# Strassen's seven products in the gated MLP of a hybrid encoder block on one core

## The chip, the core and the metric

The kernel runs on one core of a Trainium2 chip. The metric is the time of one execution on the device, in microseconds (us). The core has a matrix engine (TensorE, PE in the profile), three engines for elementwise work (VectorE or DVE, ScalarE or ACT, GpSimd or POOL), and DMA queues; here nearly all DMAs are issued by SyncE (SP). SBUF is the memory on the core, 128 partitions wide; PSUM holds the results of PE; DRAM lies outside. An engine runs its instructions in the order in which the program lists them, and waits on semaphores for the others.

## The reference

```
h = rmsnorm(x, norm_mix_g);  z = h @ w_in              # conv heads and latent attention
x = x + concat([y_conv, y_mla]) @ w_o
hf = rmsnorm(x, norm_ffn_g)
a  = dwconv_centred(hf @ w_up, ffn_conv_w, ffn_conv_b) # width 3, over positions
g, u = split(a, 2)
x  = x + (silu(g) * u) @ w_down
gate = sigmoid(rmsnorm(x, ple_norm_g) @ w_ple_gate)
x  = x + gate * (p @ w_ple_proj)
return rmsnorm(x, final_norm_g)
```

There are 1024 positions and 1024 channels. The MLP's inner width is 2816, so 22 chunks of 128 channels for g and 22 for u. The embedding p has 256 channels. Everything is float32.

## The kernel before

Activations lie with channels on the partitions and positions along the row: one tile is 128 channels by 1024 positions. Every matrix product is made of three passes over split operands. A weight w is split into a rounded part wh and the rest wl, an activation x into xh and xl, and a product is wh·xh + wh·xl + wl·xh (`gemm`, L127 to L134: L130, L132, L134). A matmul covers 128 by 128 weights and 512 positions. `load_unit` (L119) brings 1024 columns of weights from DRAM by a DMA of SP (L116), and splits them: ACT writes wh (L123), POOL the difference wl (L124). Three raw buffers let these run ahead of PE.

After the attention, its half of the output projection is made for each of eight chunks of channels, `out_mla`; DVE adds it to x (L555), ACT and DVE split the gained x (not yet normed) into hh and hl (L213, L214), and ACT and POOL gather the squares for the norm (L221, L222). `rbc` (L158) turns the sum of squares into the factor r2 by two matmuls with ones (L170, L171) and rsqrt steps on ACT and DVE (L151 to L156).

The MLP then runs without DRAM in between. For chunk c, `ff_chunk` makes two units of 48 matmuls, g and u, on hh and hl. PE does not need r2: DVE multiplies the PSUM result by it (L226), then come the width-3 convolution (ACT L203, DVE L204 and L205), silu on ACT (L574), and the product g·u on DVE (L577). The product is split by ACT and POOL (L209, L210) into guh and gul, which stay in SBUF. The down projection takes chunks in groups, GROUPS = [4, 4, 4, 4, 3, 3]: when a group and one further chunk have been made, eight blocks of n × 6 matmuls follow, one for each output chunk, and DVE adds each into x (L625). In the last group x is split again (L213, L214) for the gate.

The last stage works on parts of the positions, (0, 512), (512, 768), (768, 1024). For each output chunk PE makes the embedding projection (12 matmuls) and the gate (24 matmuls), then ACT, DVE and POOL apply the sigmoid, the sum and the final norm. The order of instructions on each engine comes from the order of the code, a scheduler, and the buffers of the pools, and is fixed when the program is built.

Of the kernel before, what the change touches and what calls it, by code (L numbers as in the profile page):

```python
# [14 lines left out]
P = 128  # L15
S = 1024
# [3 lines left out]
NFF = 22  # L20
EPS = 1e-6
SCALE = 96.0 ** -0.5
GROUPS = [4, 4, 4, 4, 3, 3]

POOLW = 256
ACTN = (0, 3, 6)
# [7 lines left out]
def tile_block(ctx, tc, xT, pT, wlat, wun, wdn, wuq, wukv, vecs, cst, out):  # L34
# [16 lines left out]
    ps = ctx.enter_context(tc.tile_pool(name="ps", bufs=2, space=bass.MemoryType.PSUM))  # L51
# [59 lines left out]
    def vc(i):  # L111
        return vec[:, i:i + 1]
# [11 lines left out]
        ptt(out=wl, in0=raw, in1=f(wh), op=ALU.subtract)  # L124
        return wh, wl

    def gemm(acc, wh, wl, xh, xl, first, last, sl=HALF):  # L127
        hv = acc if isinstance(acc, list) else halves(acc)
        for p, s in zip(hv, sl):
            mm(p, wh, xh[:, s], start=first, stop=False)  # L130
        for p, s in zip(hv, sl):
            mm(p, wh, xl[:, s], start=False, stop=False)  # L132
        for p, s in zip(hv, sl):
            mm(p, wl, xh[:, s], start=False, stop=last)  # L134
# [89 lines left out]
    def times(out_, acc, b):  # L224
        for p, s in pieces(acc):
            tt(out=out_[:, s], in0=p, in1=b[:, s], op=ALU.mult)  # L226

# [134 lines left out]
    yp, y_done = pool("yp", "right")  # L362
    atp, at_done = pool("atp", "right")
    YH = [yp.tile([P, S], FR, name=f"ymh{i}") for i in range(4)]
# [166 lines left out]
    xp, x_done = pool("xp", "left")  # L531
    x1 = [xp.tile([P, S], F32, name=f"x{c}") for c in range(NC_)]
    for d in range(NC_):
        nc.sync.dma_start(out=x1[d], in_=x1d[d])
# [11 lines left out]
    out_mla(1, [0, 1, 2])  # L546
    values(NT // 2 - 1)
    out_mla(2, [0, 1, 2])
    ss = xp.tile([P, S], F32, name="ss")
    hh = [xp.tile([P, S], FR, name=f"hh{c}") for c in range(NC_)]  # L550
    hl = [xp.tile([P, S], FR, name=f"hl{c}") for c in range(NC_)]
    for d in range(NC_):
        out_mla(d, [3] if d < 3 else [0, 1, 2, 3])
        for p, s in pieces(accs[d]):
            tt(out=x1[d][:, s], in0=p, in1=x1[d][:, s], op=ALU.add)  # L555
# [5 lines left out]
    gp, g_done = pool("gp", "right", 6)  # L561
    tmpb, tmpb_done = pool("tmpb", "right", 4)
    tpools = [tmp, tmpb]
    cnt = [0]

    r2 = [None]
    pend = []

    def ff_evac(c, j, acc, ab):
        a = ft()  # L570
        times(a, acc, r2[0])
        ab.append(conv3(a, V_FW + 3 * (2 * c + j), V_FB + 2 * c + j))
        if j == 0:
            act(out=ab[0], in_=ab[0], func=AF.Silu)  # L574
        else:
            g, u = ab
            tt(out=g, in0=g, in1=u, op=ALU.mult)  # L577
# [5 lines left out]
    def ff_chunk(c):
        ab = []
        tpool[0] = tmpb if c % 2 else tmp
        for j in range(2):
            acc = unit_gemm(U_UP + 2 * c + j, hh, hl, [small(), small()] if c == 1 and j == 0 else None)
            if r2[0] is None:
                pend.append((c, j, acc, ab))
            else:  # L590
                ff_evac(c, j, acc, ab)

    def set_r2(r):
        r2[0] = r
        while pend:
            ff_evac(*pend.pop(0))

    ph, wj = [], []

    def prep(src, lst):  # L600
        raw = load_raw(src)
        pair = (gp.tile([P, S], FR, name="guh"), gp.tile([P, S], FR, name="gul"))
        split(raw, *pair, nc.vector)
        lst.append(pair)

    done = {}
    rbc(ss, D, xp.tile([P, S], F32, name="rbc"), 9.0, set_r2)
    nxt = 0
    col = 0
    c0 = 0  # L610
    for g, n in enumerate(GROUPS):
        last = g == len(GROUPS) - 1
        ahead = c0 + n + 1 if g < len(GROUPS) - 2 else NFF
        while nxt < ahead:
            ff_chunk(nxt)
            nxt += 1
        for d in range(NC_):
            if last and d in (0, 1, 3):
                prep(*[(pT[0], ph), (pT[1], ph), None, (wun[U_PROJ], wj)][d])
            if d % 2 == 0:  # L620
                w = load_unit(wdn[:, col:col + 2 * n * P], 2 * n * P)
                col += 2 * n * P
            p = big()
            blocks(p, w, d % 2 * n, [done[c0 + k][0] for k in range(n)], [done[c0 + k][1] for k in range(n)], range(n), n)
            tt(out=x1[d], in0=p, in1=x1[d], op=ALU.add)  # L625
            if last:
                if d == 0:
                    ss = xp.tile([P, S], F32, name="ss")
                    hh, hl = [], []
                hh.append(xp.tile([P, S], FR, name=f"hh{d}"))  # L630
                hl.append(xp.tile([P, S], FR, name=f"hl{d}"))
                split_gain(x1[d], vc(V_PLE + d), hh[d], hl[d])
                square_acc(ss, x1[d], d == 0)
        c0 += n

# [1 line left out]
    prep(wun[U_PROJ + 1], wj)  # L637
    r3 = [None]
    gate_pend = []
    last_sq = []  # L640
    PARTS = [(0, 512), (512, 768), (768, 1024)]
    sf = [xp.tile([P, b - a], F32, name=f"sf{i}") for i, (a, b) in enumerate(PARTS)]

    def gate_evac(i, d, pg, pj):
        a, b = PARTS[i]
# [53 lines left out]
    rbc(ss, D, xp.tile([P, S], F32, name="rbc"), 8.0, set_r3)  # L699
    for i, (a, b) in enumerate(PARTS):  # L700
        s = slice(a, b)
        for d in range(NC_):
            w = load_unit(wun[U_GATE + d])
            if i == 0 and d in (2, 3):
                pg, pj = small(), small()
            elif i == 0:
                p = big()
                pg, pj = p[:, 0:512], p[:, 512:1024]
            else:
                p = small()  # L710
                pg, pj = p[:, 0:256], p[:, 256:512]
            for k in range(2):
                c = slice((d % 4 * 2 + k) * P, (d % 4 * 2 + k) * P + P)
                gemm([pj], wj[d // 4][0][:, c], wj[d // 4][1][:, c], ph[k][0], ph[k][1], k == 0, k == 1, [s])
            for k in range(NC_):
                c = slice(k * P, k * P + P)
                gemm([pg], w[0][:, c], w[1][:, c], hh[k], hl[k], k == 0, k == NC_ - 1, [s])
            if r3[0] is None:
                gate_pend.append((i, d, pg, pj))
            else:  # L720
                gate_evac(i, d, pg, pj)
        if b < S:
# [114 lines left out]
```

## Time and profile before

| | |
|---|---|
| median of three runs | 1410.96 us (1410.74 to 1413.64) |
| span of the profiled execution | 1409.6 us |
| instructions | 16320, of which 6612 matmuls |
| PE, DVE, ACT, POOL busy | 97%, 57%, 39%, 40% |
| the MLP (first matmul on hh to the first of the gate stage) | 528.0 to 1254.3 us |
| the gate stage | 1254.3 to 1409.6 us |

The page of the profile gives busy times, slices of the span, groups of instructions by line (busy time in us, mean of one in ns, then the idle time ahead of them and what ended it) and DMA issues. In rows of the timeline stand start, duration, engine, line, operation, output<-input and, in brackets, the idle time before it with its releaser. A row of the windows view gives a stretch, its length and the busy time of each engine with the number of instructions.

### The profile page before, as it was taken

To read this page: it belongs to the slowest core of one execution; us is meant where nothing else is said; L and a number is where in the kernel's file an instruction comes from. 1 tells how busy PE (TensorE), PEld (TensorE's weight loads), DVE (VectorE), ACT (ScalarE), POOL (GpSimd) and SP (SyncE) were. 2 spreads that over 40 slices of the span, in tenths; PEclk is the share of its full clock that TensorE was granted. 3 is DMA by queue.
4 is the path that set the end of the run, shared out by engine and by line. 5 is a ranking of instruction groups with operands and counts; after the bars stand their busy time and mean duration, and the time that the engine had idled before them with its cause. 6 is when DMAs were issued, how large, how long until landed. Compare 5 with 4: busy or idle time off the path is not lost.

```text
span 1409.6 us, 16320 instructions
## 1 busy us (share of the span) xinstructions
PE 1369.1 (97%) x6612; PEld 1140.1 (81%) x6612; DVE 809.1 (57%) x918; ACT 548.0 (39%) x737; POOL 570.8 (40%) x331
## 2 busy tenths in 40 slices
PE   7999999999999999999999999999999999989976
PEld 5878788888888888888888888888888888868876
DVE  7478824799998667443244234423441444477786
ACT  4223322788888554331132123202221232244433
POOL 5266552455556373432232223422322232282443
PEclk9999999999999999999999999999999999999987
DMA  5211134200001211111111111111111111321242
GB/s 185 82 45 45 45 128 148 69 1 16 1 16 46 90 45 46 47 58 45 45 46 55 51 45 46 45 49 56 45 46 45 57 41 38 93 80 67 91 153 87
DMA packets 27227, 85.90 MB, mean 61 GB/s; under 512 B 2960, under 2 KB 6288, under 8 KB 27152
## 3 DMA queue, kind: packets, MB, share of 16 engines
q1 hardware_dynamic: 26464, 84.23, 18.2%
q8 instruction: 52, 0.85, 0.3%
q10 hardware_dynamic: 688, 0.64, 0.1%
q14 instruction: 23, 0.19, 0.0%
HBM read 76.46 MB, written 8.39 MB: 60 GB/s over the span
## 4 chain that ended last, share of the span: by engine, by line
PE 87%; DVE 7%; issue 2%; ACT 1%; POOL 1%; DMA 1%; POOLq 0%; SPq 0%; ACTq 0%; DVEq 0%
PE big L132 22%; PE big L134 22%; PE big L130 22%; PE small L471 4%; PE small L484 2%; PE big L441 2%; PE big L443 2%; PE big L445 2%; PE small L483 2%; PE small L130 2%; PE small L132 2%; PE small L134 2%; DVE x L654 1%; DVE x L672 1%; DVE hl L214 1%
## 5 line engine op out<-in xcount | busy, mean ns | idle before, releaser
L124 POOL TENSOR_TENSOR wlo<-wraw,whi 128x1024 fp32r<-128x1024 f32 (+2 forms) x116 | 276.6, 2385 | 535.0 <-ACT whi L123 534.7
L130 PE MATMUL big<-hh,whi 128*128 128x512 f32 x960 | 303.8, 393 | 5.6 <-DVE hh L262 5.6
L134 PE MATMUL big<-hh,wlo 128*128 128x512 f32 x960 | 303.4, 393 | 2.6 <-DVE wlo L267 2.6
L132 PE MATMUL big<-hl,whi 128*128 128x512 f32 x960 | 303.6, 393 | 1.2 <-DVE hl L214 1.2
L123 ACT ACTIVATE whi<-wraw 128x1024 fp32r<-128x1024 f32 (+2 forms) x116 | 119.3, 1028 | 375.6 <-PE big L132 331.3
L130 PEld LDWEIGHTS big<-hh,whi 128*128 128x128 f32 x960 | 181.3, 189 | 46.0 <-DVE hh L262 6.1
L134 PEld LDWEIGHTS big<-hh,wlo 128*128 128x128 f32 x960 | 181.7, 189 | 42.4 <-DVE wlo L267 3.0
L132 PEld LDWEIGHTS big<-hl,whi 128*128 128x128 f32 x960 | 181.5, 189 | 41.8 <-DVE hl L214 1.7
L226 DVE TENSOR_TENSOR tmp<-big,rbc 128x1024 f32<-128x1024 f32 x47 | 57.5, 1224 | 214.7 <-PE big L134 214.5
L625 DVE TENSOR_TENSOR x<-big,x 128x1024 f32<-128x1024 f32 x48 | 58.7, 1223 | 134.5 <-PE big L134 134.2
L204 DVE SCALAR_TENSOR_TENSOR tmp<-tmp,vec 128x1023 f32<-128x1023 f32 x48 | 81.9, 1708 | 60.8 <-ACT tmp L203 57.2
L134 PE MATMUL big<-guh,wlo 128*128 128x512 f32 x352 | 110.6, 395 | 0.0
L132 PE MATMUL big<-gul,whi 128*128 128x512 f32 x352 | 110.6, 395 | 0.0
L130 PE MATMUL big<-guh,whi 128*128 128x512 f32 x352 | 110.6, 395 | 0.0
L458 POOL TENSOR_SCALAR tmp<-tmp,sm 128x256 f32<-128x256 f32 x64 | 71.0, 1109 | 94.8 <-DVE sm L451 94.8
L210 POOL TENSOR_TENSOR gul<-tmp,guh 128x1024 fp32r<-128x1024 f32 x22 | 52.6, 2391 | 109.5 <-ACT guh L209 109.5
L448 DVE TENSOR_REDUCE mx<-big 128x1 f32<-128x1024 f32 x64 | 78.0, 1219 | 11.5 <-PE big L445 11.0
L474 DVE TENSOR_TENSOR ptl<-small,pth 128x512 fp32r<-128x512 f32 x128 | 83.3, 679 | 1.0 <-ACT pth L473 0.7
L132 PEld LDWEIGHTS big<-gul,whi 128*128 128x128 f32 x352 | 66.0, 187 | 16.2
L134 PEld LDWEIGHTS big<-guh,wlo 128*128 128x128 f32 x352 | 66.0, 187 | 16.2
L130 PEld LDWEIGHTS big<-guh,whi 128*128 128x128 f32 x352 | 66.0, 187 | 16.1
L473 ACT CAST pth<-small 128x512 fp32r<-128x512 f32 x128 | 68.9, 592 | 19.5 <-PE small L471 17.1
(222 smaller groups left out, 2220.6 us busy)
## 6 DMA issues: line engine op xcount, KB each, us to landing
wraw<-in_wun_dram SPq DMA_DIRECT2D x90, 512.0 KB, 3.3
wraw<-in_wdn_dram SPq DMA_DIRECT2D x16, 512.0 KB, 3.7
tmp<-in_xT_dram SPq DMA_DIRECT2D x15, 512.0 KB, 4.3
x1d<-tmp SPq DMA_DIRECT2D x8, 512.0 KB, 2.9
x<-x1d SPq DMA_DIRECT2D x8, 512.0 KB, 7.3
wraw<-in_wdn_dram SPq DMA_DIRECT2D x8, 384.0 KB, 3.2
out_dram<-x SPq DMA_DIRECT2D x8, 256.0 KB, 3.3
wraw<-in_wlat_dram SPq DMA_DIRECT2D x8, 224.0 KB, 3.8
```

Source lines behind the costliest of these rows:

```text
L123: act(out=wh, in_=raw, func=AF.Copy)
L124: ptt(out=wl, in0=raw, in1=f(wh), op=ALU.subtract)
L130: mm(p, wh, xh[:, s], start=first, stop=False)
L132: mm(p, wh, xl[:, s], start=False, stop=False)
L134: mm(p, wl, xh[:, s], start=False, stop=last)
L204: stt(out=t[:, 1:S], in0=src[:, 0:S - 1], scalar=vc(w), in1=t[:, 1:S], op0=ALU.mult, op1=ALU.add)
L226: tt(out=out_[:, s], in0=p, in1=b[:, s], op=ALU.mult)
L448: nc.vector.tensor_reduce(m, p, AX.X, ALU.max, negate=True)
L458: nc.gpsimd.tensor_scalar(out=e[:, w:S], in0=e[:, w:S], scalar1=su, scalar2=None, op0=ALU.mult)
L473: nc.scalar.copy(out=pth[:, ks, qs], in_=t)
L474: tt(out=ptl[:, ks, qs], in0=t, in1=f(pth)[:, ks, qs], op=ALU.subtract)
L625: tt(out=x1[d], in0=p, in1=x1[d], op=ALU.add)
```

## The change

In the MLP the two matrix products are made by Strassen's scheme in Winograd's form: 2 × 2 blocks are multiplied with seven products of blocks, not eight, for which sums and differences of blocks are formed first and results are summed afterwards. (Line numbers below are those of the changed kernel.)

**Up.** The blocks are two halves of the input channels, the two halves of the positions (T1S, T2S) and the pair g and u. A unit of the changed kernel is the g and the u chunk of one c: seven steps of 4 × 3 = 12 matmuls on 512 positions (`Unit`). `stationary` (L603) makes the weight blocks a11, a12, a22 and s1 to s4: ACT copies (L610), DVE differences (L611), DVE sums (L619 to L623), and one difference on POOL (a22). `up_moving` (L672) makes the input blocks b11, b21, b22 and t1 to t4 once, from the normed input: DVE norms eight tiles (L683), ACT copies (L678), DVE takes differences (L679, L689, L697, L701, L702). So r2 is needed before the first product. The steps are run in the order 1, then 4 of the previous unit, then 6, 5, 2, 7, 3; the first two units are run side by side. Steps 1 and 2 share a PSUM bank, as do 6, 7, 4 and 5, 3: the first result of a bank is read (L731, or ACT L737) before the next step is added on top of it. After the convolution (L207 to L209), silu and product (L751), the chunk is written to DRAM (gud, L752).

**Between.** x1 is written to DRAM before the MLP (x2d, L563), since its buffers are reworked, and is read back (L777) when the buffers of up are given up.

**Down.** Pairs of chunks are the inner blocks, in groups DGROUPS = [3, 3, 3, 2] of pairs. For a group, `group_moving` loads the products (L789) and `moving` (L580) makes the blocks (L586 on ACT, L587 and L597 to L601 on DVE), in rings of 8 narrow (e1) and 21 wide (e2) buffers. A unit makes two output chunks in seven steps of n × 3 matmuls; DVE adds each into x (L803), step 1 into a tile g1 that is added at the end of the last group.

**The embedding projection** is moved from the gate stage to the place ahead of the up products (L710 to L720), is written to DRAM (pjd) and read back for each part (L909).

The diff, cut to its core:

```
-GROUPS = [4, 4, 4, 4, 3, 3]
+DGROUPS = [3, 3, 3, 2]
...
+    def moving(y1, y2, one, two):
...
+        put(["b11"], y1[:, T1S], one, 1)
+        put(["b21", "b22"], y2, two, 2)
+        tt(out=y1[:, T1S], in0=y1[:, T2S], in1=y1[:, T1S], op=sub)
+        tt(out=y1[:, T2S], in0=y2[:, T2S], in1=y1[:, T2S], op=sub)
+        put(["t1", "t3"], y1, two, 2)
+        tt(out=y2[:, T2S], in0=y2[:, T2S], in1=y1[:, T1S], op=sub)
+        tt(out=y2[:, T1S], in0=y2[:, T1S], in1=y2[:, T2S], op=sub)
+        put(["t4", "t2"], y2, two, 2)
...
+    def stationary(g, u, n, mid, mk):
...
+        put(["a11", "a12"], g, w2("whi"), w2("wlo"), nc.vector)
+        tt(out=s14[:, lo], in0=u[:, lo], in1=u[:, hi], op=ALU.add)
+        tt(out=s23[:, lo], in0=s14[:, lo], in1=g[:, lo], op=ALU.subtract)
+        tt(out=s14[:, hi], in0=g[:, hi], in1=s23[:, lo], op=ALU.subtract)
+        put(["s1", "s4"], s14, mid(2), mid(2), nc.vector)
+        tt(out=s23[:, hi], in0=g[:, lo], in1=u[:, lo], op=ALU.subtract)
+        put(["s2", "s3"], s23, mid(2), mid(2), nc.vector)
+        put(["a22"], u[:, hi], mid(1), mid(1), nc.gpsimd)
...
+    TERMS = {1: ("a11", "b11"), 2: ("a12", "b21"), 3: ("s4", "b22"), 4: ("a22", "t4"),
+             5: ("s1", "t1"), 6: ("s2", "t2"), 7: ("s3", "t3")}
+    BANK = {1: 0, 2: 0, 6: 1, 7: 1, 4: 1, 5: 2, 3: 2}
+    FIRST = (1, 6, 5)
...
+    def run(unit):
+        for i in (1, 6, 5, 2, 7, 3):
+            unit.step(i)
+            if i == 1 and held[0]:
+                held[0].step(4)
+        held[0] = unit
...
+    rbc(ss, D, plp.tile([P, S], F32, name="rbc"), 9.0, up_moving)
+    for d in range(NC_):
...
+        nc.sync.dma_start(out=pjd[d], in_=t)
...
+    for c in range(2, NFF):
+        run(up_unit(c))
+    run_last()
...
+        nc.sync.dma_start(out=x1[d], in_=x2d[d])
...
+    e1 = lambda: bxp.tile([P, 512], FR, name="e1", bufs=8)
+    e2 = lambda: bxp.tile([P, S], FR, name="e2", bufs=21)
...
+    for gi, n in enumerate(DGROUPS):
+        bs = group_moving(range(q0, q0 + n))
+        for j in range(4):
+            run(down_unit(col, range(q0, q0 + n), bs, j, gi))
+            col += 4 * n * P
+        q0 += n
+    run_last()
...
-            for k in range(2):
-                c = slice((d % 4 * 2 + k) * P, (d % 4 * 2 + k) * P + P)
-                gemm([pj], wj[d // 4][0][:, c], wj[d // 4][1][:, c], ph[k][0], ph[k][1], k == 0, k == 1, [s])
```

The order of instructions moves at two places that matter below. The first is VectorE at the beginning of the MLP. Before, when the rsqrt steps (L155, L156) have given r2 (rbc), PSUM results that are already there are multiplied by it:

```order
L155 SCALAR_TENSOR_TENSOR tmp<-tmp,ss 128x512
L156 SCALAR_TENSOR_TENSOR rbc<-tmp,rbc 128x512
L226 TENSOR_TENSOR tmp<-big,rbc 128x1024 x2
L204 SCALAR_TENSOR_TENSOR tmp<-tmp,vec 128x1023 x2
L205 SCALAR_TENSOR_TENSOR tmp<-tmp,vec 128x1023 x2
L577 TENSOR_TENSOR tmp<-tmp 128x1024
```

Now the norm of the eight input tiles (xt) stands there, then the differences that make the low parts of b11 (b_4968 to b_4983):

```order
L160 SCALAR_TENSOR_TENSOR rbc<-tmp,rbc 128x512
L611 TENSOR_TENSOR wlo<-wraw,whi 128x1024
L683 SCALAR_TENSOR_TENSOR xt<-xt,vec,rbc 128x1024 x8
L679 TENSOR_TENSOR b_4968<-xt,b_4967 128x512
L679 TENSOR_TENSOR b_4973<-xt,b_4972 128x512
L679 TENSOR_TENSOR b_4978<-xt,b_4977 128x512
L679 TENSOR_TENSOR b_4983<-xt,b_4982 128x512
```

The multiplication by r2 has moved from behind the products to a place ahead of all of them.

The second is VectorE in the down projection. Before, the adds of a group into x (L625) stand one behind the other, and then the next up unit's work:

```order
L625 TENSOR_TENSOR x_4529<-big,x_4529 128x1024
L625 TENSOR_TENSOR x_4530<-big,x_4530 128x1024
L625 TENSOR_TENSOR x_4531<-big,x_4531 128x1024
L226 TENSOR_TENSOR tmp<-big,rbc 128x1024
L204 SCALAR_TENSOR_TENSOR tmp<-tmp,vec 128x1023
```

Now, at the border between the first and the second group, it reads as follows; x_8095 and x_8096 are the last outputs of the first group, e_8589 to e_8637 low parts of operands for the second group (e_8627 is the b11 of its third pair, with which its first product ends), wlo and wm its weights, and g_8105 takes its first product:

```order
L587 TENSOR_TENSOR e_8589<-tmp,e_8588 128x1024
L611 TENSOR_TENSOR wlo<-wraw,whi 128x768
L587 TENSOR_TENSOR e_8595<-tmp,e_8594 128x1024
L803 TENSOR_TENSOR x_8096<-bk,x_8096 128x512
L611 TENSOR_TENSOR wm_8665<-s_8655,wm_8664 128x768
L587 TENSOR_TENSOR e_8607<-tmp,e_8606 128x1024
L803 TENSOR_TENSOR x_8095<-bk,x_8095 128x512
L587 TENSOR_TENSOR e_8613<-tmp,e_8612 128x1024
L587 TENSOR_TENSOR e_8627<-tmp,e_8626 128x512
```

Operands of the next group have come in between the last reads of the group before, and the b11 of the third pair stands behind all of them.

More of the change, by code (lines that the diff above doesn't have):

```diff
@@ L583, in ff_chunk @@
[L583 to L589, printed above, removed]
-            else:
[L591 to L604, printed above, removed]
@@ L606, in tile_block @@
-    done = {}
-    rbc(ss, D, xp.tile([P, S], F32, name="rbc"), 9.0, set_r2)
-    nxt = 0
-    col = 0
[L610 to L634, printed above, removed]
@@ L637, in tile_block, with bank @@
-    prep(wun[U_PROJ + 1], wj)
+        nc.sync.dma_start(out=x2d[d], in_=x1[d])
+        if d in (3, 4):
+            raw = load_raw(pT[d - 3])
+            ph.append((plp.tile([P, S], FR, name=f"pth{d}"), plp.tile([P, S], FR, name=f"ptl{d}")))
+            split(raw, *ph[-1])
+    y_done()
+    ps_done()
+    pb = ctx.enter_context(tc.tile_pool(name="pb", bufs=8, space=bass.MemoryType.PSUM, reuse_waits="tile"))
+    def bank():
+        return pb.tile([P, 512], F32, name="bk")
+    smallf[0] = bank
@@ new lines, in tile_block, with __init__, step @@
+    FULL = [slice(0, 512)]
+    TERMS = {1: ("a11", "b11"), 2: ("a12", "b21"), 3: ("s4", "b22"), 4: ("a22", "t4"),
+             5: ("s1", "t1"), 6: ("s2", "t2"), 7: ("s3", "t3")}
+    BANK = {1: 0, 2: 0, 6: 1, 7: 1, 4: 1, 5: 2, 3: 2}
+    FIRST = (1, 6, 5)
+    class Unit:
+        def __init__(self, a, bs, read):
+            self.a, self.bs, self.read, self.banks = a, bs, read, {}
+        def step(self, i):
+            m = BANK[i]
+            if i in FIRST:
+                self.banks[m] = bank()
+            p = self.banks[m]
+            wh, wl = self.a[TERMS[i][0]]
+            n = len(self.bs)
+            for k, b in enumerate(self.bs):
+                c = slice(k * P, k * P + P)
+                xh, xl = b[TERMS[i][1]]
+                gemm([p], wh[:, c], wl[:, c], xh, xl, i in FIRST and k == 0, k == n - 1, FULL, i not in FIRST)
+            self.read(i, p)
@@ new lines, in tile_block @@
+    rbc(ss, D, plp.tile([P, S], F32, name="rbc"), 9.0, up_moving)
+    for d in range(NC_):
+        if d % 4 == 0:
+            wj = load_unit(wun[U_PROJ + d // 4])
+        acc = [bank(), bank()]
+        for k in range(2):
+            c = slice((d % 4 * 2 + k) * P, (d % 4 * 2 + k) * P + P)
+            gemm(acc, wj[0][:, c], wj[1][:, c], ph[k][0], ph[k][1], k == 0, k == 1)
+        t = ft()
+        for p, s in pieces(acc):
+            nc.scalar.copy(out=t[:, s], in_=p)
+        nc.sync.dma_start(out=pjd[d], in_=t)
@@ new lines, in tile_block, with up_unit, read @@
+    pl_done()
+    tmpb, tmpb_done = pool("tmpb", "left", 4)
+    def up_unit(c):
+        raws = [load_raw(wun[U_UP + 2 * c + j]) for j in range(2)]
+        mid = lambda n: sp.tile([P, n * 512], FR, name=f"wm{n}", bufs=6 if n == 2 else 4)
+        a = stationary(raws[0], raws[1], 512, mid, lambda m: sp.tile([P, S], F32, name=m))
+        ag, au = tmp.tile([P, S], F32, name="tmp"), tmp.tile([P, S], F32, name="tmp")
+        add = lambda o, p, q: tt(out=o, in0=p, in1=q, op=ALU.add)
+        out_, half = [], []
+        def read(i, p):
+            g1, g2, u1, u2 = ag[:, T1S], ag[:, T2S], au[:, T1S], au[:, T2S]
+            if i == 1:
+                nc.scalar.copy(out=u1, in_=p)
+            elif i == 5:
+                add(u2, p, u1)
+            elif i == 2:
+                nc.scalar.copy(out=g1, in_=p)
+            elif i == 7:
+                add(u2, p, u2)
+            elif i in (3, 6):
+                add(g2, p, g2 if half else u1)
+                half.append(i)
+            else:
+                add(u1, p, u1)
+                tpool[0] = tmpb
+                t = conv3(au, V_FW + 6 * c + 3, V_FB + 2 * c + 1)
+                tt(out=t, in0=out_[0], in1=t, op=ALU.mult)
+                nc.sync.dma_start(out=gud[c], in_=t)
+            if i in (3, 6) and len(half) == 2:
+                tpool[0] = tmpb
+                t = conv3(ag, V_FW + 6 * c, V_FB + 2 * c)
+                act(out=t, in_=t, func=AF.Silu)
+                out_.append(t)
+        return Unit(a, hf, read)
@@ new lines, in tile_block @@
+    pair = [up_unit(0), up_unit(1)]
+    for i in (1, 5, 2, 3, 6, 7, 4):
+        for unit in pair:
+            unit.step(i)
+    for c in range(2, NFF):
+        run(up_unit(c))
+    run_last()
+    tmpb_done()
+    s_done()
+    xt_done()
+    bx_done()
+    tpool[0] = tmp
+    xp, x_done = pool("xp", "left")
+    x1 = [xp.tile([P, S], F32, name=f"x{c}") for c in range(NC_)]
+    for d in range(NC_):
+        nc.sync.dma_start(out=x1[d], in_=x2d[d])
+    g1s = [xp.tile([P, 512], F32, name=f"g{j}") for j in range(4)]
@@ new lines, in tile_block, with group_moving @@
+    sp, s_done = pool("sq", "left")
+    bxp, bx_done = pool("by", "right")
+    e1 = lambda: bxp.tile([P, 512], FR, name="e1", bufs=8)
+    e2 = lambda: bxp.tile([P, S], FR, name="e2", bufs=21)
+    def group_moving(pairs):
+        bs = []
+        for q in pairs:
+            y = [tmp.tile([P, S], F32, name="tmp") for _ in range(2)]
+            for j in range(2):
+                nc.sync.dma_start(out=y[j], in_=gud[2 * q + j])
+            bs.append(moving(y[0], y[1], e1, e2))
+        return bs
```

179 lines of the change are left out of this document (132 added, 47 removed).

## The prediction

> **What bounds the kernel now.** I read the page first, then a table of windows over the two stages that the change touches.
>
> ```profile
> PE 1369.1 (97%) x6612; PEld 1140.1 (81%) x6612; DVE 809.1 (57%) x918; ACT 548.0 (39%) x737; POOL 570.8 (40%) x331
> ...
> PE   7999999999999999999999999999999999989976
> ...
> DVE  7478824799998667443244234423441444477786
> ```
>
> ```profile
> 528.00:1254.30 726.30, 726.30 (x3173) 595.21 (x3172) 298.71 (x232) 197.40 (x185) 230.67 (x97) 1.00 0.16 50
> 1254.30:1409.60 155.30, 127.61 (x741) 113.05 (x739) 119.31 (x161) 60.54 (x97) 65.84 (x28) 0.91 0.29 99
> 1320.00:1380.00 60.00, 49.26 (x360) 47.12 (x360) 52.15 (x75) 25.23 (x46) 27.98 (x12) 0.91 0.39 136
> ```
>
> The columns after the length are the busy time of PE, PEld, DVE, ACT and POOL, the granted clock and DMA. From 528.0 to 1254.3, the MLP, PE has no idle time at all; DVE works 299 of 726 us. Then comes the gate stage, 155.3 us, where PE is idle for 28 us and, from 1320 on, DVE (52.15 of 60) is busier than PE (49.26). So matmuls removed from the MLP count in full, as long as the DVE work that replaces them, and the waits on it, stay under PE's time.
>
> The pitch of PE comes from the DVE's starts behind it.
>
> ```profile
> 660.45 1.22 DVE L625 TENSOR_TENSOR x<-big,x 128x1024 f32<-128x1024 f32 x1 [4.38 <-PE big L134]
> 666.05 1.22 DVE L625 TENSOR_TENSOR x<-big,x 128x1024 f32<-128x1024 f32 x1 [4.38 <-PE big L134]
> ...
> 715.53 1.23 DVE L226 TENSOR_TENSOR tmp<-big,rbc 128x1024 f32<-128x1024 f32 x1 [4.08 <-PE big L134]
> ...
> 726.41 1.23 DVE L226 TENSOR_TENSOR tmp<-big,rbc 128x1024 f32<-128x1024 f32 x1 [5.34 <-PE big L134]
> ```
>
> An up unit of 48 matmuls takes 726.41 − 715.53 = 10.88 us, 0.2267 each; a down block of 24 takes 666.05 − 660.45 = 5.60, 0.2333 each.
>
> **What the change removes.** Before: 44 up units × 10.88 = 478.7, down 44 × 5.60 = 246.4 (1056 matmuls), together 725.1 of the 726.3. After: 22 up units × 7 products × 4 × 3 = 1848 matmuls and 16 down units, 924. The new operands lie elsewhere, so either pitch could hold; I take the dearer 0.2333: up 431.1 (19.6 a unit), down 215.6, together 646.7. That saves 79.6 us; at 0.2267 it would be 98.
>
> **The projection, moved.** 96 matmuls and 4 of the norm's reduction are now ahead of the up products: 100 × 0.2333 = 23 us, so PE is through at 528 + 23 = 551. It takes the same out of the gate stage, but that stage waits for DVE in its second half, and DVE keeps its work there (the projection is now read from SBUF). I give 9 us back of 155.3, 146 left; bounds 0 and 20. Its eight stores and loads are 0.5 MB and less each, in queues with 84% of room.
>
> **The DVE prices.**
>
> ```profile
> L474 DVE TENSOR_TENSOR ptl<-small,pth 128x512 fp32r<-128x512 f32 x128 | 83.3, 679 | 1.0 <-ACT pth L473 0.7
> ...
> L205 DVE SCALAR_TENSOR_TENSOR tmp<-tmp,vec 128x1023 f32<-128x1023 f32 x48 | 65.6, 1368 | 1.6
> ...
> L577 DVE TENSOR_TENSOR tmp<-tmp 128x1024 f32<-128x1024 f32 x22 | 26.9, 1224 | 1.9 <-ACT tmp L574 1.3
> ...
> L209 ACT CAST guh<-tmp 128x1024 fp32r<-128x1024 f32 x22 | 23.1, 1049 | 92.5 <-DVE tmp L577 92.5
> ...
> L298 DVE SCALAR_TENSOR_TENSOR rawq<-rawq,vec,rbc 128x1024 f32<-128x1024 f32 x2 | 2.5, 1282 | 0.0
> ```
>
> With some 0.04 between instructions I use 0.73 for 512 elements, 1.26 for 1024, 1.0 for 768 between them, 1.31 for the scaled form on 1024, and 1.05 for an ACT copy of 1024.
>
> **An up unit in the steady state.** DVE has five reads of 512 (3.65), three splits of 1024 (3.8), four sums (2.9), four scaled adds (5.3) and a product (1.26): 16.9 us against PE's 19.6. POOL keeps one split of 512. PE's shared banks need a read of step 6 before step 7, two steps of 2.8 us later, so 5.6 us of cover. I cost waits there at nothing; the cover is the 2.7 us a unit by which DVE is ahead. If it goes, DVE sets the pace (rival).
>
> **A: the start of up.** The products take the normed input, so now PE waits for r2; before, the norm came after the matmuls.
>
> ```profile
> 528.24 1.23 DVE L555 TENSOR_TENSOR x<-big,x 128x1024 f32<-128x1024 f32 x1 [1.83 <-PE big L134]
> ...
> 535.46 1.22 DVE L163 TENSOR_TENSOR tmp<-ss,tmp 128x1024 fp32r<-128x1024 f32 x1
> ...
> 550.80 0.69 DVE L156 SCALAR_TENSOR_TENSOR rbc<-tmp,rbc 128x512 f32<-128x512 f32 x1
> ```
>
> r2 was ready at 551.5. Now ACT has weight copies between its squares: 554 (551.5 to 557). In the order DVE then does all eight norms, 8 × 1.31 = 10.5, before the first split: 564.5; the first b11 is there at 565.2, 14 us after PE is free. Four splits of b21, four differences and one more follow (t1 from 576.9 to 581.2), so step 5 of the first pair ends at 584.7; steps 2 and 3 run to 595.9. The t2 splits end at 600.3; steps 6, 7 and 4 then take to 615. Without waits two units would end at 551 + 39.2 = 590. Stall A: 25 us (18 to 34).
>
> **C: from up to down.** The last up products are released only after T, PE's end of up. Until then the space of x1 is not free, so eight loads of x2d start behind T, and the second unit's weights and the gated pairs queue behind them on SP.
>
> ```profile
> 453.17 4.07 SPq L534 DMA_DIRECT2D x<-x1d  x8
> ```
>
> ```profile
> wraw<-in_wun_dram SPq DMA_DIRECT2D x90, 512.0 KB, 3.3
> wraw<-in_wdn_dram SPq DMA_DIRECT2D x16, 512.0 KB, 3.7
> ...
> x<-x1d SPq DMA_DIRECT2D x8, 512.0 KB, 7.3
> ```
>
> The like transfer here was issued over 4.07 us and took 7.3 us to land. DVE is in order: it reads the last step, makes the last gated product (some 6 us), then stands at the difference of the second unit's weights until about T + 10. Five instructions for that unit (4), then the pairs: b11 of the first at T + 16, of the second at T + 20, the third waits for a buffer of the first, 3.3 to 3.7 us of load, and T + 30. Its chain of differences, copies and splits, about 13 us, gives its t2 at T + 43. Steps 6, 5, 2, 7, 3 of 9 matmuls (2.1 each) follow: T + 54 where 12.6 would do. Stall C: 41 us (24 to 48).
>
> **D: between groups.** A group of three needs 18 wide buffers out of 21, so most of the next group's operands are written when the last unit of this group lets go. The order has the b11 of the third pair behind splits that wait for that unit's step 7. With E the end of its last step, these splits and the reads between them (1.26, 1.0, 1.26, 0.73, 1.0, 1.26, 0.73, 1.26, 0.73, from E − 3.5) give E + 5.8, where PE wants it at E + 1.4: 4.4. Step 6 then wants t2 of all three pairs, twenty DVE instructions further, E + 23; its end is E + 23.7 for 6.3. That is 17 us, at two borders; at the third (a group of two) 8 (3 to 12). Bounds at the first two: 4 (only the first piece) and 24. In the last group a unit has 42 matmuls, 9.8 us, and DVE seven adds, three more for g1, two scaled splits and its weights' work, 13.7: 4 × 3.9, of which I take 12 (4 to 16). D: 17 + 17 + 8 + 12 = 54.
>
> **The clock after a stall.**
>
> ```profile
> 1269.83 0.63 PE L170 MATMUL small<-tmp,onesr 128*128 128x512 f32 x1
> 1270.25 0.63 PE L171 MATMUL small<-tmp,onesr 128*128 128x512 f32 x1
> ...
> 1272.71 0.40 PE L134 MATMUL big<-hh,wlo 128*128 128x512 f32 x1
> 1272.94 0.39 PE L130 MATMUL big<-hh,whi 128*128 128x512 f32 x1
> ```
>
> This stretch follows PE's longest gap at the gate's norm: matmuls stand 0.42 apart until 1272.7, 0.23 afterwards. About 3 us at that pitch lose 1.4 us. Six stalls (two in A, one in C, three in D): 8 us (4 to 12). [...]
>
> **The sum.** 528 + 23 + 431.1 + 25 + 215.6 + 41 + 54 + 8 = 1325.7 for the end of down, and 146: 1471.7 of span, 62 over 1409.6. The median of the runs is 1.4 over the profiled span: 1473 us, 4.4% slower. A measurement of this kernel can tell about 0.2% from no change, 1408 to 1414.
>
> **Rivals.**
> *The waits overlap; faster.* Each wait shows only its first piece: A 14 (the r2 wait), C 24, D 4.4 + 4.4, clock 4, so 51: 528 + 23 + 646.7 + 51 + 146 = 1395 of span, 1396. For it: PE had nearly no waits before and DVE has 2.7 us to spare per unit. Against: DVE's order is fixed, and b11 and t2 stand in it where I have them. It turns where all stalls are under half of my 128.
> *DVE sets up's pace; slower still.* The scaled adds were dearer beside POOL:
>
> ```profile
> L204 DVE SCALAR_TENSOR_TENSOR tmp<-tmp,vec 128x1023 f32<-128x1023 f32 x48 | 81.9, 1708 | 60.8 <-ACT tmp L203 57.2
> ...
> L203 ACT ACTIVATE tmp<-tmp,vec 128x1024 f32<-128x1024 f32 x44 | 54.6, 1243 | 26.1 <-DVE tmp L226 26.1
> ...
> L574 ACT ACTIVATE tmp<-tmp 128x1024 f32<-128x1024 f32 x22 | 23.3, 1061 | 67.4 <-DVE tmp L205 67.4
> ```
>
> With two at 1.75 a unit has 17.7 us of DVE; with the ACT steps before the adds and the product uncovered (1.24 each, and the silu 1.06: 3.6) it is 21.3, past 19.6 from 2 us uncovered on: 20 units × 1.9 = 38, 1511. [...]
> *Nothing gained.* Stalls of about 66 us would cancel saving and move: 1411. That the products are not fewer can be excluded: PE's list has 6216 matmuls for 6612.
>
> **How the numbers follow.** My forecast with its bounds 0.66; overlap 0.16, DVE's pace 0.13, no change 0.05. Faster 0.16, same 0.05, slower 0.79. All bounds low at once, 0.2267 included, give 1377; all high, 1524. The range leaves out the overlap case and what lies over DVE's pace: 1400 to 1515.
>
> **What would show it.** In the profile after: PE idle from about 551 to 565 behind DVE's L683 (right for A); L611 or L587 with a DMA as releaser after the last L752, and about 40 us of idle PE (C); PE waits on L587 at three places in down (D); starts of L751 about 19.6 us apart (up bound by PE; over 20.5, the second rival). I am wrong if PE's idle time between 528 and the gate is under 60 us, or if the gate stage shrinks by over 20.

## The result and the profile after

The changed kernel takes 1462.87 us (median of four runs, 1459.73 to 1465.16), the kernel before 1411.2 in runs on the same chip: a ratio of 1.0357, 95% interval 1.0338 to 1.0375. The change costs 3.6%; 1473 us had been forecast, and a range of 1400 to 1515.

The page of the changed kernel, busy times first, then three rows of the slices:

```profile
PE 1317.7 (90%) x6168; PEld 1073.4 (73%) x6168; DVE 1137.2 (78%) x1441; ACT 654.4 (45%) x919; POOL 413.9 (28%) x283
...
PE   7999999999999995999999999995596969879865
...
DVE  7578734899898369988888888876868787898896
...
PEclk9999999999999997999999999998698989999977
```

PE has 51 us less to do (1369.1 before), the span is 53 us longer. The gaps stand where the prediction put them: at slice 16, the start of up; from slice 28, the border to down; and three times behind it. DVE has gone from 809 to 1137 us.

The windows view of the changed kernel gives a row to each stage: the projection, the first two up units, the other twenty, the first down unit, the rest of down, and the gate stage. The columns are length, busy time of PE, PEld, DVE, ACT and POOL with the number of instructions, granted clock, DMA share and GB/s.

```profile
528.05:556.70 28.65, 25.05 (x101) 19.65 (x99) 22.60 (x28) 17.86 (x29) 7.55 (x4) 0.94 0.52 194
556.70:615.80 59.10, 43.47 (x169) 33.34 (x169) 58.08 (x73) 31.17 (x39) 2.01 (x1) 0.86 0.10 37
615.80:1005.60 389.80, 389.80 (x1681) 314.96 (x1679) 311.01 (x333) 158.87 (x178) 25.05 (x20) 1.00 0.24 84
1005.60:1058.05 52.45, 20.23 (x55) 12.84 (x55) 42.57 (x55) 20.55 (x24) 2.76 (x2) 0.61 0.54 194
1058.05:1311.70 253.65, 214.54 (x871) 166.54 (x870) 200.16 (x274) 79.73 (x101) 36.01 (x21) 0.94 0.23 70
1311.70:1462.20 150.50, 111.67 (x597) 96.23 (x595) 122.56 (x162) 61.22 (x97) 63.08 (x28) 0.86 0.37 123
```

The third row is Strassen as it was meant: for 390 us PE has no idle time, twenty units take 19.49 us each, and DVE works 311 us beside it. In the second and fourth row it is PE that is idle, and the clock is granted at 0.86 and 0.61. In the waits of PE (engine, line, who is waited for: us in total, times, longest) the first entries of before were 6.1 and 5.9 us; now they are

```profile
PE bk L134 <- ACT e L586: 52.6, 11, 17.6
PE bk L138 <- POOL wlo L128: 12.9, 10, 2.1
PE bk L136 <- DVE e L587: 11.0, 11, 2.6
PE bk L136 <- DVE b L679: 10.4, 3, 7.5
```

L586 and L587 make the blocks of the down projection, L679 those of up.

Against the terms of the prediction, in us of the profiled execution:

| stage | forecast | measured |
|---|---|---|
| embedding projection ahead | 23 | 28.65 |
| first two up units (39 without waits; A 25, clock 2.8) | 67 | 59.1 |
| twenty up units | 392 | 389.8 |
| first down unit (12.6; C 41, clock 1.4) | 55 | 52.45 |
| rest of down (203; D 54, clock 4.2) | 261 | 253.65 |
| gate stage | 146 | 150.5 |

With the 528.05 us ahead, the measured column gives the span of 1462.2.

### The profile page after: what moved, and what is told of

It reads as the page before. It is cut to its first block, busy times and chain, and to the rows that moved or that the text cites. A ratio compares the mean times of both kernels' runs of the same rounds, so it can differ in the third digit from the quotient of the medians.

```text
span 1462.2 us, 16476 instructions
## 1 busy us (share of the span) xinstructions
PE 1317.7 (90%) x6168; PEld 1073.4 (73%) x6168; DVE 1137.2 (78%) x1441; ACT 654.4 (45%) x919; POOL 413.9 (28%) x283
## 5 line engine op out<-in xcount | busy, mean ns | idle before, releaser
L611 POOL TENSOR_TENSOR wm<-wraw,wm 128x512 fp32r<-128x512 f32 (+2 forms) x38 | 48.7, 1282 | 695.3 <-ACT wm L610 618.9
L128 POOL TENSOR_TENSOR wlo<-wraw,whi 128x1024 fp32r<-128x1024 f32 (+1 forms) x50 | 123.6, 2475 | 146.2 <-ACT whi L127 140.0
L134 PE MATMUL bk<-e,whi 128*128 128x512 f32 (+1 forms) x280 | 102.8, 367 | 27.8 <-ACT e L586 24.1
L134 PE MATMUL bk<-e,wm 128*128 128x512 f32 x220 | 92.2, 419 | 36.2 <-ACT e L586 28.5
L610 ACT CAST whi<-wraw 128x1024 fp32r<-128x1024 f32 (+2 forms) x38 | 35.6, 936 | 181.3 <-PE bk L136 181.3
L138 PE MATMUL bk<-e,wlo 128*128 128x512 f32 (+1 forms) x280 | 103.2, 368 | 12.9 <-POOL wlo L128 12.9
L610 ACT CAST wm<-s 128x1024 fp32r<-128x1024 f32 (+2 forms) x76 | 70.8, 932 | 89.9 <-PE bk L136 54.9
L136 PE MATMUL bk<-e,whi 128*128 128x512 f32 (+1 forms) x280 | 102.3, 365 | 7.9 <-DVE e L587 6.6
L136 PE MATMUL bk<-b,wm 128*128 128x512 f32 x264 | 105.2, 399 | 2.9 <-DVE b L679 2.9
L134 PE MATMUL bk<-b,wm 128*128 128x512 f32 x264 | 104.9, 397 | 0.0
L138 PE MATMUL bk<-b,wm 128*128 128x512 f32 x264 | 104.9, 397 | 0.0
L803 DVE TENSOR_TENSOR x<-bk,x 128x512 f32<-128x512 f32 x96 | 65.3, 686 | 48.0 <-PE bk L138 47.7
L731 DVE TENSOR_TENSOR tmp<-bk,tmp 128x512 f32<-128x512 f32 x110 | 75.5, 686 | 29.4 <-PE bk L138 29.4
L136 PE MATMUL bk<-e,wm 128*128 128x512 f32 x220 | 91.5, 416 | 4.4 <-DVE e L587 4.4
L611 DVE TENSOR_TENSOR wm<-s,wm 128x1024 fp32r<-128x1024 f32 (+2 forms) x76 | 84.1, 1107 | 8.0 <-ACT wm L610 7.8
L138 PE MATMUL bk<-e,wm 128*128 128x512 f32 x220 | 90.2, 410 | 0.0
L207 ACT ACTIVATE tmp<-tmp,vec 128x1024 f32<-128x1024 f32 x44 | 54.4, 1237 | 74.3 <-DVE tmp L731 74.2
L452 DVE TENSOR_REDUCE mx<-big 128x1 f32<-128x1024 f32 x64 | 78.0, 1219 | 11.6 <-PE big L449 11.1
L134 PEld LDWEIGHTS bk<-e,whi 128*128 128x128 f32 x280 | 57.9, 207 | 37.8 <-ACT e L586 26.1
```

What stands on the lines that cost most here:

```text
L134: mm(p, wh, xh[:, s], start=first, stop=False, skip_group_check=more)
L136: mm(p, wh, xl[:, s], start=False, stop=False, skip_group_check=more)
L138: mm(p, wl, xh[:, s], start=False, stop=last, skip_group_check=more)
L452: nc.vector.tensor_reduce(m, p, AX.X, ALU.max, negate=True)
L610: nc.scalar.copy(out=h, in_=src)
L611: eng.tensor_tensor(out=z, in0=src, in1=f(h), op=ALU.subtract)
```

## The experiments

Times are ratios to the kernel before, run on the same chip. The start of the MLP lay between 527 and 533 us in the profiles, with the same code ahead of it (proj_gate apart), so stages are compared by their own lengths. In the excerpts of the edits "..." stands for lines that are not shown, and words after # are mine.

**Strassen in up alone** (up_only). The gated products still go through DRAM; the down projection is the ordinary one.

```
-    bs = group_moving(range(q0, q0 + n)) ... down_unit(...)
+    for g, n in enumerate([4, 4, 4, 4, 3, 3]):
+        ...                              # load gud[c0 + k], split on ACT and DVE
+        blocks(p, w, d % 2 * n, ...); tt(out=x1[d], in0=p, in1=x1[d])
```

> Strassen is kept in the up projection and undone in the down projection: the gated products still go through DRAM, but the down projection has the ordinary products again (1056 matmuls for 924, 246 us for 216), and VectorE makes one low part per chunk instead of the pairs' sums and differences. Theory (the change loses its gain in the waits on VectorE's block sums at the border to down and between groups): down costs 31 us more of matmuls, the wait at the border shrinks from 40 to about 8 us, the 51 us lost between groups go: about 1411 us, as fast as before. Rival (the way through DRAM and the reload of x is what costs): the border stays at 25 us or more and the total at 1430 or above. Rival (up itself brings no gain): 1440 or above.

Measured: 1.007 (1.0044 to 1.0096). 2.9% of the 3.6% went, so most of the loss is in the down half (Strassen in down alone was not run); up with its r2 wait costs less than 1%. The forecast, as fast as before, was missed by 0.7%, 10 us; 7 of them are the border, where PE waited 15 us, not 8:

```profile
1012.90 1.22 PE L134 MATMUL bk<-guh,whi 128*128 128x512 f32 x2 [4.56 <-ACT guh L213]
1024.29 1.22 PE L136 MATMUL bk<-gul,whi 128*128 128x512 f32 x2 [10.17 <-DVE gul L214]
```

From there to the gate it has no wait worth naming.

**The first group's blocks for all groups** (reuse).

```
-        bs = group_moving(range(q0, q0 + n))
+        bs = bs[:n] if gi else group_moving(range(q0, q0 + n))
```

> The second to fourth group of the down projection use the first group's blocks again: their loads, copies, sums and differences are left out (part of the computation is left out), every matmul, read and weight stays. Theory (borders wait for those blocks): the waits of 12.3, 12.7 and 6.1 us and the slow clock behind them, about 9 us, go: 40 us less, about 1423 us. Rival (VectorE's reads and weight sums pace the down projection, whatever stands at the borders): the waits turn up elsewhere and 15 us or less go, 1448 or above.

Measured: 1.007 (1.0044 to 1.0096), 40 us less than the full change, the theory's number. The rest of down, in the changed kernel and then in this one:

```profile
1058.05:1311.70 253.65, 214.54 (x871) 166.54 (x870) 200.16 (x274) 79.73 (x101) 36.01 (x21) 0.94 0.23 70
1058.80:1275.50 216.70, 207.81 (x870) 164.89 (x869) 157.61 (x215) 53.78 (x72) 34.74 (x21) 0.98 0.17 54
```

216.7 us for 253.65, with PE busy for all but 9. Reads and weight sums alone, 158 us of DVE, hold PE up only in the last group, where those 9 us stand (the waits are on L803). At the borders it is the making of the next group's blocks that does.

**The products with the last block last** (t2_last, then t2_mid).

```
-            run(down_unit(col, range(q0, q0 + n), bs, j, gi))
+            run(down_unit(...), (1, 6, 5, 2, 7, 3) if j else (1, 2, 5, 3, 6, 7))   # t2_last
+            run(down_unit(...), (1, 6, 5, 2, 7, 3) if j else (1, 2, 5, 6, 3, 7))   # t2_mid
```

> Only the order of the seven products in the first unit of each group changes: 1, 2, 5, 3, 6, 7 instead of 1, 6, 5, 2, 7, 3, so that the products with t2 and t4, the blocks that are ready last, come last. Theory (a border waits for the last block, not for VectorE's total work): about 6 us less at the border from up to down, 6, 6 and 5 at the borders between groups, with some of the slow clock: 24 us less, about 1439. Rival (VectorE's work in the down stage is the bound, so that a wait moved away comes back later): less than 5 us, 1458 or above.

> Like t2_last, but the first unit of each group runs 1, 2, 5, 6, 3, 7: in t2_last steps 6 and 7, which share a PSUM bank, stood side by side and TensorE waited for the read between them (six waits of 1 to 2 us at the borders); here another step lies between. Theory (order sets the border, and t2_last lost its gain to those reads): 15 us less than the full change, a ratio of 1.025. Rival (VectorE's total work in the down stage is the bound): the waits turn up at the next reads, as in t2_last: 5 us less or nothing, 1.032 to 1.036.

t2_last measured 1.0324 (1.0296 to 1.0352), 5 us less: the number of the rival, but not for its reason. In the changed kernel the first border between groups has these waits of PE:

```profile
1106.97 0.50 PE L136 MATMUL bk<-e,whi 128*128 128x512 f32 x1 [2.59 <-DVE e L587]
...
1111.86 0.51 PE L134 MATMUL bk<-e,wm 128*128 128x512 f32 x1 [1.35 <-ACT e L586]
...
1113.39 0.50 PE L136 MATMUL bk<-e,wm 128*128 128x512 f32 x1 [1.02 <-DVE e L587]
...
1121.03 0.79 PE L134 MATMUL bk<-e,wm 128*128 128x512 f32 x1 [6.91 <-ACT e L586]
1122.30 0.79 PE L136 MATMUL bk<-e,wm 128*128 128x512 f32 x1 [0.47 <-DVE e L587]
```

The long one, 6.91, is the t2 of the third pair. In t2_last it is gone, and new ones stand behind it, for a read that nothing covers any more:

```profile
1128.06 0.50 PE L134 MATMUL bk<-e,wm 128*128 128x512 f32 x1 [1.23 <-DVE x L803]
1134.20 0.50 PE L134 MATMUL bk<-e,wm 128*128 128x512 f32 x1 [1.69 <-DVE x L803]
```

Steps 6 and 7 share a bank and had become neighbours. With step 3 between them (t2_mid) the ratio is 1.0262 (1.024 to 1.0284), 13 us less than the full change where the theory said 15. At the same border t2_mid has

```profile
1113.27 0.50 PE L136 MATMUL bk<-e,whi 128*128 128x512 f32 x1 [2.38 <-DVE e L587]
...
1119.36 0.50 PE L134 MATMUL bk<-e,wm 128*128 128x512 f32 x1 [0.31 <-ACT e L586]
```

and no read. So the order in which blocks become ready, against the order in which they are used, is a cause of its own, and DVE's total work not yet a bound.

**The norm on halves** (half_norm).

```
         for k in range(4):
-            norm(k)
+            norm(k, T1S)
...
         for k in range(4):
+            norm(k, T2S)
```

> At the start of up the norm of the first four tiles is made on halves of the positions, so that b11 is there after four short instructions instead of eight long ones; nothing else changes. Reading 1 (the order of the eight norms costs): TensorE's first wait of 7.5 us behind them goes, 7 us less, 1456. Reading 2 (VectorE's whole chain up to t2 sets the end of the first pair; in the profile the last t2 is ready under 1 us before its matmul): TensorE starts some 7 us sooner and waits that much longer at t1 and t2, within 2 us of 1463. I hold reading 2 the likelier.

Measured: 1.0391 (1.036 to 1.0422), not faster, its interval overlapping the full change's. The waits of PE at the start of up, in the changed kernel and then in this one:

```profile
561.47 0.80 PE L134 MATMUL bk<-b,whi 128*128 128x512 f32 x1 [4.75 <-ACT b L678]
569.79 0.79 PE L136 MATMUL bk<-b,whi 128*128 128x512 f32 x1 [7.53 <-DVE b L679]
579.76 0.74 PE L136 MATMUL bk<-b,wm 128*128 128x512 f32 x1 [2.65 <-DVE b L679]
```

```profile
562.93 0.49 PE L134 MATMUL bk<-b,whi 128*128 128x512 f32 x1 [2.17 <-ACT b L678]
565.62 0.80 PE L136 MATMUL bk<-b,whi 128*128 128x512 f32 x1 [2.19 <-DVE b L679]
573.66 0.80 PE L136 MATMUL bk<-b,whi 128*128 128x512 f32 x1 [3.84 <-DVE b L679]
584.22 0.80 PE L136 MATMUL bk<-b,wm 128*128 128x512 f32 x1 [4.88 <-DVE b L679]
```

The wait of 7.53 is gone and comes back in pieces. From the end of the projection to the third up unit both take 59 us. Reading 2 holds for this stage: it is DVE's whole chain that sets the end (58.08 of 59.10 us busy in the second stage above). The total is 6 us higher than the full change's where reading 2 allowed 2; in the profiled executions 3 us of the difference lie ahead of the MLP and 4 in down and the gate stage, whose source is the same.

**The projection back in the gate stage** (proj_gate).

```
-    for d in range(NC_): ... nc.sync.dma_start(out=pjd[d], in_=t)
...
+                gemm([pj], wj[d // 4][0][:, c], wj[d // 4][1][:, c], ph[k][0][h], ph[k][1][h], k == 0, k == 1, [s0])
```

> One part undone: the embedding projection is made in the gate stage again, not ahead of the up products. Theory (it fills a time in which TensorE waits for r2 anyway, and the gate stage has VectorE as its bound): TensorE stands idle from the end of the output projection until the first b11, which comes some 3 to 5 us sooner, and the gate stage takes 5 to 10 us more: between 5 us less and 5 us more than the full change, a ratio of 1.032 to 1.039. Rival (the 28 us at the front are a cost of their own): 18 us less or more, 1.023.

Measured: 1.0437 (1.0415 to 1.046), 11 us slower than the full change; both expectations missed. From the end of the output projection to the end of up it takes 464.4 us for 477.4, so only 13 of the projection's 28.65 us cost anything there; and the output projection itself now takes 4 us longer, since PE waits 3.8 us in it for DVE's adds (L561). The rest covered the r2 chain:

```profile
539.12 0.76 PE L174 MATMUL bk<-tmp,onesr 128*128 128x512 f32 x1 [5.77 <-DVE tmp L166]
...
553.62 0.79 PE L134 MATMUL bk<-b,whi 128*128 128x512 f32 x1 [11.69 <-ACT b L673]
```

But the gate stage takes 162 us for 150.5, and down some 6 more: PE has one wait of 6.6 us for a read of the last group; what made that read late was not separated. Moving the projection was worth its price.

**The border to down** (late_x2d, x2d_after).

```
-        nc.sync.dma_start(out=x1[d], in_=x2d[d])
+        nc.scalar.dma_start(out=x1[d], in_=x2d[d])                                   # late_x2d
...
+                nc.gpsimd.tensor_copy(out=x1[d][:, 0:1], in_=f(bs[-1]["b22"][0])[:, 0:1])   # x2d_after
+                nc.sync.dma_start(out=x1[d], in_=x2d[d])
```

> The full change, with the reload of x1 issued by ScalarE's queue, so that weights and gated products of the down projection no longer stand behind it. Theory of the border (C) as predicted: the wait of VectorE for the second unit's weights (3.5 us) goes and the pairs come earlier: 4 to 8 us less, a ratio of 1.030 to 1.033. Rival (VectorE's chain of the three pairs sets the border, whatever comes first): within 2 us of the full change, 1.034 to 1.037.

> The full change, with the reload of x1 made to wait (one element of each tile is written first by GpSimd, from the third pair's b22) until the first group's products have been loaded. In late_x2d the reload was in another queue, but the DMA engines still moved about 400 GB/s from 4 to 22 us after up's end, and the weights and pairs came as late as before. Theory (the border waits for 4.2 MB of transfers, 10 us at that rate): the first product starts some 8 us sooner and the border loses 8 us: a ratio of 1.030. Rival (VectorE's chain of the three pairs sets the border): within 2 us of the full change, 1.034 to 1.037.

late_x2d measured 1.0355 (1.0328 to 1.0381): nothing. The DMA view of that kernel from 1000 to 1045 us, in 40 equal slices:

```profile
GB/s 302 211 408 11 0 0 0 0 98 382 411 248 350 382 401 408 422 406 374 413 409 360 314 396 335 295 123 5 0 0 0 0 0 175 291 18 291 171 0 280
```

From 1010 to 1030 the engines carry 250 to 420 GB/s. The other queue did not get the weights past the 4.2 MB that were on their way: ACT waits 5.83 us for those of the second unit, 5.97 in the changed kernel. With the reload held back (x2d_after, 1.0323, 1.0304 to 1.0342) the first product starts 8.1 us after up's end, for 17.6:

```profile
1013.92 0.79 PE L134 MATMUL bk<-e,whi 128*128 128x512 f32 x1 [8.11 <-ACT e L586]
```

Of these 9.5 us 4.4 are kept (from the end of up to the gate 301.7 us for 306.1). The rest is waited for later, in DVE's chain of the three pairs: from up's end to the last t2 it takes 35.8 us, for 40.8 in the changed kernel, of which DVE is busy for 34.2 (its work in the whole of down is 243.2 us, for 242.7). Both causes of C in the prediction are real, the chain the larger.

**Three edits together** (small_mid): x2d_after, t2_mid, and

```
-DGROUPS = [3, 3, 3, 2]
+DGROUPS = [2, 3, 3, 3]
```

> The full change with three edits: the order 1, 2, 5, 6, 3, 7 at the borders (t2_mid, ratio 1.026), the reload of x1 made to wait (x2d_after), and DGROUPS = [2, 3, 3, 3], so that the first group needs two pairs only and the last group's units have 14.7 us of matmuls for VectorE's 13 or so. Theory (each border waits for its own last block and its own transfers, so that the gains add): 8 us less for the reload and 7 for the third pair's chain: a ratio of 1.016. Rival (VectorE's work, the same in sum, is by now the bound of the down stage): 1.021 or above.

Measured: 1.0158 (1.0124 to 1.0191), the theory's number: 28 us less than the full change. That the number came is in part luck: x2d_after had kept under 5 us of the 8 counted for the reload, and the regrouping was not run alone, so how the 28 us divide is not shown. Down takes 276 us for 306. Waits of up to 3.4 us at the borders between groups are left, and one of 11.6 at the border to down.

**Up alone, with its border mended** (up_late, up_best, up_shared). All three start from up_only.

```
+            y = hz(F32) ...                      # up_late: 16 buffers of its own; the reload of x1 is queued behind the first group's loads
+                nc.gpsimd.tensor_copy(out=x1[d][:, 0:1], in_=f(done[-1][0])[:, 0:1]) ...   # up_best: the reload waits
+            done.append((hz(), hz())) ...        # up_shared: one ring of 20 for guh, gul, hh, hl
+            split(y, *done[-1], nc.gpsimd if c0 + k < 2 else nc.vector)
```

> As up_only (Strassen in up alone), but the gated products are loaded into buffers of their own and the reload of x1 is queued behind those of the first group. In up_only TensorE waited 4.6 and 10.2 us at the border to down, behind loads that stood after the eight reloads of x1 (10 us) in the same queue. Theory (the wait at the border is that queue): the first products land 3 to 4 us after up's end and the border costs about 6 us in place of 15: 9 us less than up_only, a ratio to before of 1.000. Rival (the border waits for VectorE's last convolution and the splits behind it, some 8 us after up's end): at most 4 us less, 1.004 or above.

> Strassen in up alone (up_only), with the reload of x1 made to wait in the same way until the fourth chunk's product has been loaded. In up_only the border from up to down cost 17.5 us. Theory (transfers of the reload ahead of the products): about 8 us of border are left, 9 less than up_only, a ratio to before of 1.000: the products saved in up (50 us) just pay for the r2 wait, the border and the projection ahead. Rival (the border waits for the store of the last product and the buffers it frees): 1.005 or above.

> up_best with two edits at the border from up to down: the operands of the down projection lie in one ring of 20 buffers above the space of the last gated products (in up_best the second chunk's copy had to wait until the last product was stored, since it took over its buffer), and the low parts of the first two chunks are made by GpSimd, which is idle there. In up_best TensorE waits 4.6 and 5.7 us at this border. Theory (buffer handed over late): the second wait shrinks to 1 or 2 us, 4 us less than up_best, a ratio to before of 1.000, which is Strassen in up paying exactly for its own costs. Rival (VectorE's last convolution and product, which end some 8 us after up, set that wait): 1.003 or above.

up_late measured 1.015 (1.013 to 1.017), slower than up_only against both readings: one wait of 21.22 us for the second chunk. In that program the second chunk's copy takes over the buffer of the last gated product, so it waits until that is stored; and the store stood on SP behind the reload and six loads, issued at 1023.30. up_best measured 1.0035 (1.0022 to 1.0049), between its two expectations. Its border has 4.56 and 5.68 us of waiting. up_shared, which frees the copy from that buffer, has 4.2 in all:

```profile
1009.86 0.72 PE L136 MATMUL bk<-hz,whi 128*128 128x512 f32 x2 [1.05 <-POOL hz L214]
1013.02 0.74 PE L134 MATMUL bk<-hz,whi 128*128 128x512 f32 x2 [1.98 <-ACT hz L213]
1014.59 1.22 PE L136 MATMUL bk<-hz,whi 128*128 128x512 f32 x2 [0.83 <-DVE hz L214]
1016.97 1.22 PE L134 MATMUL bk<-hz,whi 128*128 128x512 f32 x2 [0.31 <-ACT hz L213]
```

and 0.9989 (0.9973 to 1.0006). That is level with the kernel before, and no version tried here beats that kernel. Which of up_shared's two edits did it was not separated.

## Why the prediction was right

The forecast and the mechanism held: matmuls removed count in full, and the price is paid at the start of up, at the border to down, and at each border between groups (PE's idle time between 528 and the gate is 90 us, well over the 60 that I had named). That the total came within 10 us is in part luck. PE's waits in A, C and D were forecast at 120 us and came to 87 (15.6, 32.2 and 39.1). What PE lost there beyond waits and matmuls was forecast at 8 us, at most 12, and came to 24 (4.5, 7.6 and 11.6). The clock term was too small by a factor of three, and the waits, which I had too high, more than made up for it.

*The saving.* 79.6 us forecast. Twenty units ran at 19.49 us, so up takes 428.8 us of matmuls for 478.7; the pitch of 0.232 lies between the two rows that I had (0.2267, 0.2333). Both nearly occur: from 587 to 604 us, matmuls that move b blocks stand 0.233 apart, those that move xt blocks 0.228.

*The projection.* 28.65 us for 23: PE meets the norm's own chain there (1.47 and 2.13 us of waiting) and a clock of 0.94. The gate stage gave back 4.8 us where I took 9.

*A.* 20 us with the clock's loss, for 25 and 2.8. Since DVE sets A's end, the 5.65 us more of the projection came off this wait: the first two units ended at 615.8, forecast at 615 and 2.8 for the clock. r2 was there at 558.4, later than my 554 (bound 557): DVE's weight sums (L619, L623) and ACT's copies of the projection (L719) stood between its steps. But DVE was quicker:

```profile
559.49 9.65 DVE L683 SCALAR_TENSOR_TENSOR xt<-xt,vec,rbc 128x1024 f32<-128x1024 f32 x8
569.06 5.89 DVE L679 TENSOR_TENSOR b<-xt,b 128x512 fp32r<-128x512 f32 x7
```

Eight norms in 9.65 us make 1.2 each, not 1.31; in this run an instruction starts some 0.08 us before the listed end of the one ahead, where I had added 0.04. It is also a part of why D came out high; how much was not separated.

*C.* The end of the first down unit was forecast at 54 us behind up's end (55 with the clock) and stood at 52.45. With up's end at 1005.6 these rows show the steps:

```profile
1018.89 0.56 DVE L619 TENSOR_TENSOR s<-wraw 128x384 f32<-128x384 f32 x1 [3.50 <-DMA wraw<-in_wdn_dram]
1023.22 0.79 PE L134 MATMUL bk<-e,whi 128*128 128x512 f32 x1 [17.58 <-ACT e L586]
1034.48 0.79 PE L134 MATMUL bk<-e,whi 128*128 128x512 f32 x1 [6.16 <-ACT e L586]
1046.36 0.79 PE L134 MATMUL bk<-e,wm 128*128 128x512 f32 x1 [4.54 <-ACT e L586]
```

The second unit's weights came 13 us behind up's end (forecast 10), the first product 17.6 (16), the third pair's b11 28.9 (30), its t2 40.8 (43). Of the 40 us over the matmuls' 12.6, waits are 32.2; the other 7.6 are the clock, granted at 0.50 from 1023.2 to 1051, for which I had one stall of 1.4. x2d_after showed the parts: 4.4 us go with the reload's transfers; most of the remainder is DVE's work in order and the clock.

*D.* 58 us with the clock, 50.7 measured (253.65 − 203). The waits listed at the borders are 12.3, 12.7 and 6.1 us, and 7.5 in the last group: 38.6. I had 54 for these. At the first border the third pair's b11 came 4.8 us behind the end of the last step and its t2 18.9, for 5.8 and 23. In the last group two of DVE's scaled splits (L218, at 1289.22 and 1293.14) took 3.40 and 3.47 us while POOL worked on squares (L226) and splits (L611, L128), where two with POOL idle took 1.27 and 1.28; I had not counted that. Of the 12 us beyond the waits about 8 were lost on matmuls at the slow clock, where I had 4.2, and the rest on single matmuls beside a wait. After the first border the rows read

```profile
1123.31 0.63 PE L134 MATMUL bk<-e,wm 128*128 128x512 f32 x1
1123.74 0.63 PE L136 MATMUL bk<-e,wm 128*128 128x512 f32 x1
...
1126.16 0.39 PE L136 MATMUL bk<-e,wm 128*128 128x512 f32 x1
1126.39 0.40 PE L138 MATMUL bk<-e,wm 128*128 128x512 f32 x1
```

0.43 apart until 1126, 0.23 afterwards, five us from the stall's end: the slow stretch was longer than my 3 us. The stretches behind the long waits at the three borders took some 5, 5 and 4 us, each with a wait of 0.46 or 0.47 us inside; what sets their length is not shown.

*The rivals.* DVE's pace did not bind up (389.8 of 389.8 us of PE; the starts of L751 stand 19.48 us apart): the scaled adds took 1.28 us there, not 1.75 (POOL worked beside one for 0.2 us at most; in the kernel before, from 640 to 1250 us, L204 took 1.61 to 1.96 us with POOL at work beside it, 1.28 without), and DVE's work was 15.6 us a unit for my 16.9. That rival's sum also has a slip: 21.3 less 19.6 is 1.7 a unit, not 1.9, so 34 us and 1507. The overlap did not happen; but t2_mid got 13 us of it by order alone, and small_mid 28 with the reload and the groups changed too. What no order here removed is that Strassen mixes the two halves of the positions: r2 differs by position, so the norm must come ahead of the products, and the r2 chain, which before lay behind 48 matmuls and more, lies open.

## What to carry to other kernels

A scheme that saves matmuls by sums of blocks pays on the engine that makes the sums (DVE went from 809 to 1137 us), and it pays at borders, where blocks are due in one go (waits of 15.6, 32.2 and 39.1 us here): cost each border as the chain up to the last block, less what can run before it. Put the products in the order in which their blocks are ready, but keep a step between two that share a bank, or the read between them becomes the wait (1.23 and 1.69 us in t2_last). Where PE was full, the gaps cost their length and, behind the long ones, a slow clock: 24 us beside 87 of waits, most of it matmuls 0.43 us apart for 0.23.

## What the runs showed of the hardware

- At the border to down the DMA engines moved 270 to 420 GB/s for 17 us with the reload issued by SP, and 250 to 420 for 19 us with it issued by ACT; the other queue gained nothing (ratio 1.0355 for 1.0357).
- DVE instructions on 512 elements are listed at 0.68 us and follow each other at 0.60; 1.22 and 1.14 on 1024, in unbroken runs at the start of up. A sum of listed times overstates such a run by 7 to 13%.
- PE's slow stretch after a wait of 6.9 us took some 5 us. Some shorter waits had one behind them, others not: at the first two borders between groups a wait of 2.59 us left the pitch at 0.23, but after one of 2.65 at the start of up, and after 1.47 and 2.13 close together at 539 to 542, matmuls stood 0.43 apart for some 3 us.
